# A two-layer hybrid decoder trunk on one core: limits of queued jobs, an earlier release, fixed places for two additions

## The chip, the cores and the metric

The kernel runs on one core of one Trainium2 chip. The metric is the device time of one execution in microseconds (us). Names of engines: PE is TensorE (matmul), PEld its weight load, DVE is VectorE, ACT is ScalarE, POOL is GpSimd, SP issues the DMAs.

## The reference, cut to what matters

The sequence has 256 positions of width 2048, all in float32, and there are two layers.

```
for l in range(DEPTH):
    h = rms_norm(x, mix_norm[l])
    z = h @ w_in[l]                                  # 2048 x 7168
    a_out = chunked_spatial_gating(z[..., :c_a], ...)          # gelu, layer norm, 128x128 mixing
    b_out = dilated_attention(z[..., c_a:c_q], z[..., c_q:c_k], z[..., c_k:], ...)
    mixed = concat([rms_norm(a_out, ...), rms_norm(b_out, ...)])
    x = x + mixed @ w_out[l]                         # 2048 x 2048
    h = rms_norm(x, ffn_norm[l])
    x = x + (silu(h @ w_gate[l]) * (h @ w_up[l])) @ w_down[l]  # 2048 x 5632, 5632 x 2048
```

## The kernel before, in words

Every matrix product is made at float32 accuracy from three matmuls of a rounded type: each operand is split into a high part (a copy on ACT) and a low part (source minus high part, on DVE), and `mm3` (line 837) adds high x high, high x low and low x high into one PSUM bank. The weights come from HBM as `raw` tiles by DMA and are split on the chip as well (`split_w`, line 815): tiles `wh` and `wl`, or `w` where both fit one slot. A weight item of 128 x 2048 thus takes one ACT copy and one DVE subtraction.

**Plain blocks.** The products with `w_in` and `w_out` go by blocks of 512 output columns (`plain_block`, line 844): two PSUM banks `Z`, one for each 128 positions, collect all slices of the contraction. Each slice is six matmuls. `w_out` is cut into halves "b" and "a" of the contraction; the last two blocks are (3,b) and (3,a). After each a residual operation adds the block, scaled by row, to `xs` (line 686) and gives its two banks back. After an "a" block the same job goes on: squares, transposes, and the operand of the FFN for these columns. Blocks 0 and 1 become the "forms" fF, blocks 2 and 3 the split tiles `fT`.

**Units.** The FFN's products go by `unit` (line 875). A gate/up unit makes 512 columns of gate and of up; a down unit makes two blocks of 512 columns of the result. A part of the contraction goes through a Strassen-like scheme with seven products instead of eight: seven sums of weight quarters, seven sums of operand quarters (the forms 11, 22, S1, S3, S2, 12, S4) and four banks called 1, X, Y and Z. The order of the seven is p1, p5, p6, p2, p7, p3, p4; a product has twelve matmuls in most units and six in the last chunk's down units. The tiles `e` and `raw` hold sums of weights. Between the products ACT copies banks (X from 1, Y from X, and the tiles s5 and s3, which the trace shows as `s`, as it does the silu tiles), and DVE adds s3 to Z and s5 to Y. The rest of the contraction follows as plain items of 24 matmuls that collect in the same four banks: banks 1 and X first (n = 0), then Y and Z (n = 1).

**Chunks.** The 11 blocks of the FFN's width go in chunks of 4, 4 and 3. A chunk has one gate/up unit for each block and then two down units. After a block's gate and up, ACT makes silu of the gate banks into two `t2` tiles, DVE multiplies them by the up banks, PE transposes the result (tiles `hTp`), and the transposes become the down units' operand (`Chunk.put_h`, line 705). Blocks 0 and 1 of a chunk go to a tile `xg`, and after block 1 its job makes the chunk's forms hF (and one fF) out of it, step by step (`make_forms`, line 618); for the third chunk also a rest `hR`. Blocks 2 and 3 become split tiles `hT`.

**What sets the order.** All instructions are emitted by a program that runs on the host and keeps a model of the queues (`Queues`, line 55): the time of PE, and that of ACT and DVE. Each engine then executes its own instructions in the emitted order, and only semaphores tie them together. The main loop goes through the items; before each it emits the weight preparation of later ones, as far as the ring allows (6 slots; an item takes two, or one in the last chunk's products), and then the item's matmuls. Everything else is a job, a generator that emits one step at a time. After each slice `run_jobs` looks at the jobs in the order of their limits, the highest first. A step is emitted when three things hold: the job's own model time plus 800 ns is past, its condition is met, and the backlog of ACT and DVE in the model is at most the job's limit:

```
def run_jobs(extra=0):
    for job in list(jobs):
        if job.t + MARGIN_NS <= q.pe and (job.when is None or job.when()):
            if q.backlog() <= job.limit + extra:
                job.step()
```

The limit is 4000 ns where none is given (`BACKLOG_NS`) and 30000 ns for the jobs of the FFN (`FFN_LIMIT`). Where the program needs something that a job has still to make, `drain` (line 233) moves the model's PE time on by 100 ns at a time and runs jobs until it is there. A `Lease` keeps the model's count of buffers: `mm_lease` of the four banks, `t2_lease` of the two silu tiles, `sd_lease` of the two banks for transposes.

Of the kernel before, what the change touches and what calls it, by code (L numbers as in the profile page):

```python
# [12 lines left out]
ALU = mybir.AluOpType  # L13
# [30 lines left out]
FFN_LIMIT = 30000  # L44
H_NS = 4000
MARGIN_NS = 800
BACKLOG_NS = 4000
# [95 lines left out]
def trunk_kernel(ctx: ExitStack, tc: tile.TileContext, aps: dict):  # L143
# [4 lines left out]
    dve = Engine(q, nc.vector, "dve", dve_cost)  # L148
# [52 lines left out]
    def pause(ns):  # L201
        q.chain = max(q.chain, q.pe) + ns
        yield
# [19 lines left out]
    def add(steps, limit=BACKLOG_NS):  # L223
        jobs.append(Job(steps, limit))
        jobs.sort(key=lambda job: -job.limit)
# [30 lines left out]
                    identity=ident)  # L256
        return tp

    def quad_T(src_of, put, g_of, name):

        yield from sd_lease.take(2)
        both = slot([P, 2, 4, SEQ], F32R, name)
        hi, lo = both[:, 0], both[:, 1]
        tps = [transpose_pair(src_of, 2 * pr, name + "p") for pr in range(2)]
        yield
        for pr in range(2):
            tp = tps[pr]
            if g_of is None:
                sl = slice(2 * pr, 2 * pr + 2)
                act.activation(out=hi[:, sl, :], in_=tp, func=ACTF.Copy)  # L270
                dve.tensor_tensor(
                    out=lo[:, sl, :], in0=tp, in1=hi[:, sl, :].bitcast(F32), op=ALU.subtract)
            else:
                for i in range(2):
                    k = 2 * pr + i
                    split_scaled(hi[:, k, :], lo[:, k, :], tp[:, i, :], g_of(k))
            sd_lease.give()
            if pr == 0:
                yield
        put(hi, lo)  # L280
# [318 lines left out]
        tiles = [slot([P, 2, 2, 4, P], F32R, name) for _ in range(n // 2)]  # L599
        return [t[:, h] for t in tiles for h in range(2)]  # L600

    def raw_T(src_of, dst, g_of, name):

        yield from sd_lease.take(2)
        tps = [transpose_pair(src_of, 2 * pr, name) for pr in range(2)]
        yield
        for pr in range(2):
            if g_of is None:
                act.activation(out=dst[:, 2 * pr:2 * pr + 2, :], in_=tps[pr], func=ACTF.Copy)
            else:  # L610
                for i in range(2):
                    k = 2 * pr + i
                    act.activation(
                        out=dst[:, k, :], in_=tps[pr][:, i, :], func=ACTF.Copy, scale=g_of(k))
            sd_lease.give()
            yield
# [81 lines left out]
    class Chunk:  # L698
# [3 lines left out]
            self.L, self.j0, self.n, self.s = L, j0, n, s  # L702
            self.table, self.F, self.xg = {}, None, None

        def put_h(self, j, src_of):
            i = j - self.j0
            if i >= 2:
                yield from quad_T(
                    src_of, lambda hi, lo: self.table.__setitem__(i, (hi, lo)), None, "hT")
                return  # L710
            if i == 0:
                self.xg = slot([P, 2, 4, SEQ], F32, "xg")
            yield from raw_T(src_of, self.xg[:, i], None, "hTp")
            if i == 1:
                s = self.s
                if s < 4:
                    both = slot([P, 2, 2, 4 - s, SEQ], F32R, "hR")
                    rest = self.xg[:, :, s:, :]
                    for h in range(2):
                        act.activation(out=both[:, 0, h], in_=rest[:, h], func=ACTF.Copy)  # L720
                        dve.tensor_tensor(
                            out=both[:, 1, h], in0=rest[:, h], in1=both[:, 0, h].bitcast(F32),
                            op=ALU.subtract)
                    yield
                    flat = both.rearrange("p a h k t -> p a (h k) t")
                    self.table["r"] = (flat[:, 0], flat[:, 1])
                F = Forms(form_halves(6, "hF") + [self.L.f_halves[7]], s)
                self.F = F
                yield from make_forms(F, self.xg)
# [12 lines left out]
    def gu_bank(L, j, chunk):  # L742

        s = {}

        def done(n, t, bank):
            if n == 0:
                yield lambda: hasattr(L, "r2")
                yield from t2_lease.take(1)
                s[t] = t2("s")  # L750
                act.activation(out=s[t], in_=bank, func=ACTF.Silu, scale=L.r2[:, t:t + 1])
                mm_lease.give()
                return
            yield lambda: t in s
            dve.scalar_tensor_tensor(
                out=s[t], in0=bank, scalar=L.r2[:, t:t + 1], in1=s[t], op0=ALU.mult, op1=ALU.mult)
            mm_lease.give()
            s["n"] = s.get("n", 0) + 1
            if s["n"] < NT:
                return  # L760
            yield from pause(H_NS)
            yield from chunk.put_h(j, lambda t: s[t])
            t2_lease.give(2)
        return done

    def down_bank(L, pair, chunk, last):
# [74 lines left out]
                out=out, lhsT=a, rhs=b, start=start and n == 0, stop=stop and n == 2,  # L841
                skip_group_check=True)

    def plain_block(src, kts, operand_of, done, first=None):

        st = {}
        for i in range(0, len(kts), KC):
            r = Raw([src[kts[i] // KC]], PLAIN_RAW)
            raws.append(r)
            for h in range(0, KC, HK):  # L850
                def prep(it, parts=1, r=r, h=h):
                    it.w = split_w(need(r)[:, h:h + HK, :], parts)
                    if h + HK == KC:
                        live[0] -= 1

                def run(it, i=i, h=h):
                    if i + h == 0:
                        if first is not None:
                            add(layer_consts(first), 20000)
                        drain(lambda: len(mm_lease.free) >= 2)  # L860
                        del mm_lease.free[:2]
                        st["Z"] = [mm_p.tile([P, W], F32, tag="mm", name=f"Z{t}") for t in range(NT)]
                    wh, wl = it.w
                    for k in range(HK):
                        n = i + h + k
                        for t in range(NT):
                            mm3(st["Z"][t], operand_of(kts[n], t), wh[:, k, :], wl[:, k, :],
                                n == 0, n == len(kts) - 1)
                        q.pe += 3 * NT * MM_NS
                        run_jobs()  # L870
                    if i + h + HK == len(kts):
                        add(done(st["Z"]))
                items.append(Item(1, PLAIN_RING, prep, run))

    def unit(s, quarter, plains, form, done):
# [6 lines left out]
        U = {}  # L882
# [74 lines left out]
        def r7(it):  # L957
            product(it, "S3", "X", False)
            copy(U["s3"], bank["X"])

            def sums():
                dve.tensor_tensor(out=bank["Z"], in0=bank["Z"], in1=U["s3"], op=ALU.add)
                yield lambda: "p3" in U
                yield from pause(0)
                dve.tensor_tensor(out=bank["Y"], in0=bank["Y"], in1=U["s5"], op=ALU.add)
                U["summed"] = True
            add(sums(), FFN_LIMIT)

        def r3(it):
            product(it, "S4", "Y", False)  # L970
            U["p3"] = True

        def r4(it):
            product(it, "22", "X", False)

        for p, r in ((p1, r1), (p5, r5), (p6, r6), (p2, r2), (p7, r7), (p3, r3), (p4, r4)):
            items.append(Item(1 if s <= 2 else 2, UNIT_RING, p, r))
# [3 lines left out]
        for i, (n, srcs, ops) in enumerate(plains):  # L981
            r = Raw(srcs, UNIT_RAW)
            raws.append(r)

            def prep(it, parts=1, r=r):
                it.w = split_w(need(r))
                live[0] -= 1

            def run(it, i=i, n=n, ops=ops):
                wh, wl = it.w  # L990
                for t in range(NT):
                    if n == 1:
                        drain(lambda: "summed" in U)
                    for k, op in enumerate(ops):
                        mm3(bank[names[n, t]], op(t), wh[:, k, :], wl[:, k, :], False, k == len(ops) - 1)
                        q.pe += 3 * MM_NS
                        run_jobs()
                    if i >= len(plains) - 2:
                        add(done(n, t, bank[names[n, t]]), FFN_LIMIT)
            items.append(Item(2, UNIT_RING, prep, run))  # L1000

    for l, L in enumerate(layers):
# [15 lines left out]
        for j, part in ((0, "b"), (1, "b"), (0, "a"), (1, "a"), (2, "b"), (2, "a"), (3, "b"), (3, "a")):  # L1018
            kts = list(range(8)) if part == "a" else list(range(8, 16))
            tab = operand(L.aT if part == "a" else L.bT)  # L1020
            plain_block(
                aps["w_out"][l, j], kts, (lambda kt, t, tab=tab: tab(kt % 8, t)), wout_done(L, j, part))
        j0 = 0
        for ci, (n, s) in enumerate(CHUNKS):
            chunk = Chunk(L, j0, n, s)
# [212 lines left out]
```

## Time and profile before

| | us |
|---|---|
| median of 3 runs | 2385.9 (2385.2 to 2387.07) |
| the profiled execution | 2385.62 |
| its span, first to last instruction | 2383.6 |
| PE busy | 2289.1 (96%) |
| weight load busy | 1878.5 (79%) |
| DVE busy | 1830.2 (77%) |
| ACT busy | 1325.7 (56%) |

The profile shows one execution. A busy PE includes matmuls at a lower granted clock, and the table of stretches has that clock in its own column. Line numbers of DVE and ACT instructions are those of the helper at line 90, which emits them all; the names of the tiles tell them apart (out, an arrow, in). Layer 0 runs from 0 to about 1200 us, layer 1 from there to the end; the FFN's first unit starts at 453.1 us in layer 0 and at 1644.8 us in layer 1.

### The profile page before, as it was taken

How to read it: one execution, taken by the hardware profiler on the slowest of the kernel's cores; microseconds unless marked ns; L12 is line 12 of the kernel's file. 1: busy time of each engine (PE TensorE's matmuls, PEld its weight loads, DVE VectorE, ACT ScalarE, POOL GpSimd, SP SyncE). 2: the span in 40 equal slices, each digit the busy share in tenths (PEclk: the TensorE clock that was granted, in tenths of full speed). 3: DMA queues.
4: the chain of work that ended last, by engine and by line, in shares of the span. 5: the costliest groups of instructions: out<-in, count | busy, mean ns of one | idle time of the engine just before them, and what ended most of it. 6: DMA issues, size and time to landing. Idle time of an engine off the chain costs nothing. (4 is left out here: it accounts for less than half of the span.)

```text
span 2383.6 us, 25937 instructions
## 1 busy us (share of the span) xinstructions
PE 2289.1 (96%) x10249; PEld 1878.5 (79%) x10249; DVE 1830.2 (77%) x1721; ACT 1325.7 (56%) x1590; POOL 52.5 (2%) x36
## 2 busy tenths in 40 slices
PE   9999999889999989999799999998899999899998
PEld 7888888677778878787688888886777788787876
DVE  6666766778798888988565666767787988889885
ACT  6556565455555655656355555654556556556462
POOL 0000000000000000000000000000000000000000
PEclk9999999999999999999999999999999999999999
DMA  8554455444465644645455444554445556346453
GB/s 350 185 177 159 161 201 204 155 145 159 179 227 189 228 148 160 263 159 194 163 182 196 152 162 170 195 212 158 142 159 180 226 191 228 146 161 262 159 194 106
DMA packets 66937, 440.33 MB, mean 185 GB/s; under 512 B 8064, under 2 KB 8576, under 8 KB 16768
## 3 DMA queue, kind: packets, MB, share of 16 engines
q1 hardware_dynamic: 66816, 438.69, 51.4%
q8 instruction: 80, 1.31, 0.2%
q14 instruction: 41, 0.34, 0.0%
HBM read 436.56 MB, written 2.10 MB: 184 GB/s over the span
## 5 line engine op out<-in xcount | busy, mean ns | idle before, releaser
L90 DVE TENSOR_TENSOR wl<-raw,wh 128x2048 fp32r<-128x2048 f32 x316 | 718.1, 2285 | 191.6 <-ACT wh L90 189.3
L90 ACT ACTIVATE wh<-raw 128x2048 fp32r<-128x2048 f32 x316 | 597.6, 1912 | 208.3 <-PE CX L840 76.5
L840 PE MATMUL Z<-w,xT 128*128 128x512 f32 x2688 | 640.6, 395 | 2.8 <-ACT w L90 1.5
L840 PEld LDWEIGHTS Z<-w,xT 128*128 128x128 f32 x2688 | 498.8, 188 | 106.9 <-ACT w L90 2.4
L90 DVE TENSOR_TENSOR w<-raw,w 128x1024 fp32r<-128x1024 f32 (+1 forms) x313 | 377.2, 1216 | 219.9 <-ACT w L90 215.0
L90 ACT ACTIVATE w<-raw 128x1024 fp32r<-128x1024 f32 (+1 forms) x313 | 316.2, 1049 | 47.8 <-DVE raw L90 29.5
L840 PE MATMUL CX<-wh,fF 128*128 128x512 f32 x528 | 174.8, 391 | 0.0
L840 PE MATMUL C<-wh,fF 128*128 128x512 f32 x352 | 130.0, 427 | 40.2 <-ACT s L90 23.0
L90 DVE TENSOR_TENSOR raw<-raw 128x2048 f32<-128x2048 f32 (+1 forms) x68 | 147.1, 2163 | 1.2
L840 PE MATMUL C<-wh,fT 128*128 128x512 f32 x352 | 117.3, 394 | 12.2 <-DVE fT L90 12.2
L840 PE MATMUL CY<-wh,fT 128*128 128x512 f32 x352 | 116.2, 391 | 2.7 <-DVE CY L90 2.7
L840 PEld LDWEIGHTS C<-wh,fF 128*128 128x128 f32 x352 | 72.7, 207 | 58.1 <-ACT s L90 24.7
L840 PE MATMUL CX<-wh,fT 128*128 128x512 f32 x352 | 117.6, 394 | 0.0
L840 PE MATMUL CZ<-wh,fT 128*128 128x512 f32 x352 | 115.5, 389 | 0.0
L840 PEld LDWEIGHTS CX<-wh,fF 128*128 128x128 f32 x528 | 99.2, 188 | 20.2
L840 PE MATMUL CX<-wl,fF 128*128 128x512 f32 x264 | 105.1, 398 | 4.5 <-DVE wl L90 4.4
L90 ACT ACTIVATE CX<-C 128x512 f32<-128x512 f32 x34 | 19.8, 582 | 151.7 <-PE C L840 151.7
L840 PE MATMUL Z<-w,bT 128*128 128x512 f32 x384 | 90.4, 392 | 0.0
L840 PE MATMUL Z<-w,aT 128*128 128x512 f32 x384 | 88.6, 390 | 0.0
L840 PEld LDWEIGHTS C<-wh,fT 128*128 128x128 f32 x352 | 66.8, 190 | 27.1 <-DVE fT L90 13.0
L840 PEld LDWEIGHTS Z<-w,aT 128*128 128x128 f32 x384 | 71.9, 188 | 14.9
L840 PEld LDWEIGHTS Z<-w,bT 128*128 128x128 f32 x384 | 71.7, 188 | 14.6
(192 smaller groups left out, 3554.8 us busy)
## 6 DMA issues: line engine op xcount, KB each, us to landing
raw<-in_w_in SPq DMA_DIRECT2D x109, 1024.0 KB, 4.8
raw<-in_w_gate SPq DMA_DIRECT2D x88, 1024.0 KB, 4.8
raw<-in_w_up SPq DMA_DIRECT2D x88, 1024.0 KB, 4.9
raw<-in_w_down SPq DMA_DIRECT2D x72, 1024.0 KB, 4.9
raw<-in_w_out SPq DMA_DIRECT2D x32, 1024.0 KB, 4.8
raw<-in_w_down SPq DMA_DIRECT2D x32, 512.0 KB, 4.1
raw<-in_w_in SPq DMA_DIRECT2D x5, 512.0 KB, 7.8
xstage<-in_xT SPq DMA_DIRECT2D x8, 256.0 KB, 7.3
```

Of the source, the lines that this page charges most:

```text
L90: return f(**kw)
L840: nc.tensor.matmul(out=out, lhsT=a, rhs=b, start=start and n == 0, stop=stop and n == 2, skip_group_check=True)
```

## The change

Four edits. The residual job of `w_out`, with all that follows it in the same job, gets the limit 30000 in place of 4000. `quad_T` and `raw_T` take a function `free` that they call when their transposes are emitted; the FFN's blocks give back the two silu tiles there, and not at the end of `put_h`. The job `sums` is gone: its two additions are emitted in the main order, Z's at the end of the sixth product's matmuls and Y's at the end of the seventh's. The drain that waited for the job before the plain items with n = 1 is gone with it.

```diff
-    def quad_T(src_of, put, g_of, name):
+    def quad_T(src_of, put, g_of, name, free=lambda: None):
...
         tps = [transpose_pair(src_of, 2 * pr, name + "p") for pr in range(2)]
+        free()
         yield
...
-    def raw_T(src_of, dst, g_of, name):
+    def raw_T(src_of, dst, g_of, name, free=lambda: None):
...
         tps = [transpose_pair(src_of, 2 * pr, name) for pr in range(2)]
+        free()
         yield
...
-        def put_h(self, j, src_of):
+        def put_h(self, j, src_of, free):
...
-                    src_of, lambda hi, lo: self.table.__setitem__(i, (hi, lo)), None, "hT")
+                    src_of, lambda hi, lo: self.table.__setitem__(i, (hi, lo)), None, "hT", free)
...
-            yield from raw_T(src_of, self.xg[:, i], None, "hTp")
+            yield from raw_T(src_of, self.xg[:, i], None, "hTp", free)
...
-            yield from chunk.put_h(j, lambda t: s[t])
-            t2_lease.give(2)
+            yield from chunk.put_h(j, lambda t: s[t], lambda: t2_lease.give(2))
...
-    def plain_block(src, kts, operand_of, done, first=None):
+    def plain_block(src, kts, operand_of, done, first=None, limit=BACKLOG_NS):
...
-                        add(done(st["Z"]))
+                        add(done(st["Z"]), limit)
...
             product(it, "S3", "X", False)
             copy(U["s3"], bank["X"])
 
-            def sums():
-                dve.tensor_tensor(out=bank["Z"], in0=bank["Z"], in1=U["s3"], op=ALU.add)
-                yield lambda: "p3" in U
-                yield from pause(0)
-                dve.tensor_tensor(out=bank["Y"], in0=bank["Y"], in1=U["s5"], op=ALU.add)
-                U["summed"] = True
-            add(sums(), FFN_LIMIT)
-
         def r3(it):
             product(it, "S4", "Y", False)
-            U["p3"] = True
+            w_sum(bank["Z"], bank["Z"], U["s3"], ALU.add)
 
         def r4(it):
             product(it, "22", "X", False)
+            w_sum(bank["Y"], bank["Y"], U["s5"], ALU.add)
...
-                    if n == 1:
-                        drain(lambda: "summed" in U)
...
-                aps["w_out"][l, j], kts, (lambda kt, t, tab=tab: tab(kt % 8, t)), wout_done(L, j, part))
+                aps["w_out"][l, j], kts, (lambda kt, t, tab=tab: tab(kt % 8, t)), wout_done(L, j, part),
+                limit=FFN_LIMIT)
```

`w_sum` (line 832) emits one DVE operation and leaves the model's chain time as it was.

## Rows read from the trace of the kernel before

**Rows 1.** The page, part 1: busy us (share of the span) and instructions.

```profile
PE 2289.1 (96%) x10249; PEld 1878.5 (79%) x10249; DVE 1830.2 (77%) x1721; ACT 1325.7 (56%) x1590; POOL 52.5 (2%) x36
```

**Rows 2.** List of waits of PE: us in total, times, longest.

```profile
PE C L840 <- ACT s L90: 26.2, 6, 5.8
PE CY L840 <- DVE CY L90: 19.6, 14, 5.1
PE C L840 <- DVE xs L90: 17.2, 2, 8.6
PE C L840 <- DVE fT L90: 12.2, 2, 6.1
PE CX L840 <- DVE wl L90: 7.8, 10, 0.8
```

**Rows 3.** Table of stretches: length, busy time of each engine, clock, DMA share, GB/s.

```profile
453.12:458.57 5.45, 5.45 (x13) 4.29 (x14) 1.82 (x3) 0.00 (x0) 0.00 (x0) 0.50 0.00 0
495.77:501.77 6.00, 6.00 (x17) 4.71 (x18) 0.72 (x3) 4.21 (x4) 0.70 (x1) 0.63 0.00 0
597.45:602.82 5.37, 5.37 (x13) 4.27 (x14) 1.42 (x3) 0.53 (x1) 0.00 (x0) 0.52 0.01 3
602.82:605.59 2.77, 2.77 (x13) 2.25 (x13) 0.23 (x1) 2.40 (x2) 0.00 (x0) 1.00 0.72 231
1138.69:1143.17 4.48, 4.48 (x13) 3.58 (x14) 3.34 (x3) 2.40 (x3) 0.00 (x0) 0.65 0.06 10
1169.83:1171.32 1.49, 1.49 (x6) 1.24 (x7) 0.00 (x0) 1.49 (x1) 0.00 (x0) 1.00 1.01 429
```

**Rows 4.** The same table: a unit without waits, then the one with forms.

```profile
507.05:549.04 41.99, 41.99 (x190) 34.53 (x188) 36.14 (x20) 24.70 (x19) 0.00 (x0) 1.00 0.53 188
549.04:597.45 48.41, 42.43 (x189) 34.27 (x187) 42.37 (x30) 28.28 (x26) 0.00 (x0) 0.98 0.48 174
```

**Rows 5.** DVE in order of time, FFN's entry: start, us, operation, [idle before <-releaser].

```profile
443.16 2.29 DVE L90 TENSOR_TENSOR wl<-raw,wh 128x2048 fp32r<-128x2048 f32 x1
...
446.80 0.69 DVE L90 TENSOR_TENSOR fF<-xg,fF 128x512 fp32r<-128x512 f32 x1 [0.76 <-ACT fF L90]
448.60 2.29 DVE L90 TENSOR_TENSOR wl<-raw,wh 128x2048 fp32r<-128x2048 f32 x1 [1.11 <-ACT wh L90]
...
452.23 1.40 DVE L90 SCALAR_TENSOR_TENSOR xs<-Z,rb,xs 128x512 f32<-128x512 f32 x2
453.55 1.40 DVE L90 SCALAR_TENSOR_TENSOR xs<-Z,ra,xs 128x512 f32<-128x512 f32 x2
```

**Rows 6.** DVE in order of time, before the first unit's plain items of fT.

```profile
495.24 0.48 DVE L90 SCALAR_TENSOR_TENSOR fT<-fTp,ffng,fT 128x256 fp32r<-128x256 f32 x1
496.26 0.48 DVE L90 SCALAR_TENSOR_TENSOR fT<-fTp,ffng,fT 128x256 fp32r<-128x256 f32 x1 [0.54 <-ACT fT L90]
```

**Rows 7.** DVE in order of time, between the third and fourth gate/up unit.

```profile
596.86 0.69 DVE L90 TENSOR_TENSOR fF<-xg,fF 128x512 fp32r<-128x512 f32 x1 [0.70 <-ACT fF L90]
...
598.12 0.74 DVE L90 SCALAR_TENSOR_TENSOR s<-CZ,r,s 128x512 f32<-128x512 f32 x1
605.36 2.29 DVE L90 TENSOR_TENSOR wl<-raw,wh 128x2048 fp32r<-128x2048 f32 x1 [6.49 <-ACT wh L90]
...
609.77 2.28 DVE L90 TENSOR_TENSOR wl<-e,wh 128x2048 fp32r<-128x2048 f32 x1
```

**Rows 8.** List of waits of PE from 1110 to 1190 us.

```profile
PE CY L840 <- DVE CY L90: 9.7, 2, 5.1
```

**Rows 9.** DVE in order of time, first down unit of the last chunk.

```profile
1129.86 0.69 DVE L90 TENSOR_TENSOR CZ<-CZ,s 128x512 f32<-128x512 f32 x1
...
1137.85 0.69 DVE L90 TENSOR_TENSOR CY<-CY,s 128x512 f32<-128x512 f32 x1
...
1148.66 0.69 DVE L90 TENSOR_TENSOR xs<-C,xs 128x512 f32<-128x512 f32 x1 [6.59 <-PE C L840]
```

**Rows 10.** DVE in order of time, start of the unit of 507.05 us.

```profile
512.47 2.29 DVE L90 TENSOR_TENSOR wl<-raw,wh 128x2048 fp32r<-128x2048 f32 x1 [4.25 <-ACT wh L90]
```

## The prediction, made before the changed kernel ran

> **What bounds the kernel now.** I read the page first: TensorE is busy for 96% of the span [rows 1], so what it lacks is 94.5 us. Who it waited for is told by the list of waits [rows 2]: ACT's "s" 26.2 us in 6 waits, the addition into bank Y 19.6 us in 14, the residual "xs" 17.2 us in 2, fT 12.2 us in 2. These four are 75 of the 94.5 us, and the diff touches what makes each. The third view is the table of stretches right behind such waits [rows 3]. Twelve matmuls take 2.77 us at granted clock 1.00 (2.4 GHz). Behind the 8.6 us wait for xs they take 5.45 us at clock 0.50 (1.2 GHz), behind a wait for s 5.37 us, behind a wait for bank Y 4.48 us at 0.65; behind a wait of 2.5 us six of them ran at 1.00. So each wait of some 5 us or more costs 1.7 to 2.7 us on top.
>
> The Trainium skill (Perfetto Trace Analysis, Identifying the Most-Contended Engine) says that matmul busy time is a poor measure of what TensorE could still give and that the busy share of weight loading is better. The page of the profile has 78.8% for that (1878.5 of 2383.6), a unit without waits 82.2% [rows 1, 4]. By the first measure 94.5 us are to be had; by the second 2383.6 - 1878.5 / 0.822 = 99 us. The trace has the difference in the half-clock stretches. Both stand above what I forecast.
>
> Behind TensorE stands DVE. A gate/up unit without waits takes 41.99 us with DVE busy for 36.1 of them; the unit in which a chunk's forms are made, with the wait behind it, takes 48.4, and DVE is busy for 42.4 [rows 4]. So near these waits DVE works almost without a break, and moving an operation ahead makes others late. That decides each size below.
>
> **The change, part by part.** Starts are us from the span's start, in layer 0; layer 1 has the same waits within 0.1 us unless told.
>
> *Residual at any backlog (17.2 us of wait).* At 444.5 (453.12 less 8.6) TensorE has ended w_out, and all four banks hold its last two blocks, (3,b) and (3,a). The next unit's first bank is that of (3,b), which its residual frees. This job is added when TensorE passes from (3,b) to (3,a), eight slices of six matmuls or 11 us earlier. By then DVE has been handed e, raw, wl and raw for the unit, up to the wl at 443.16 [rows 5], so the model's backlog is over 4000 ns, and the residual runs only at 452.23. With 30000 it goes in at the first step of (3,a), ahead of that wl; the last form step and half of fT's block 2, held back likewise, come along. What is late next: the second product needs the first bank of (3,a), and that residual is issued behind the wl of the third product. In DVE time from 443.2: form step 0.7 + 0.76 (wait for ACT) + 0.69, half of fT 2 x 0.48, residual (3,b) 1.40, two wl 4.58, half of residual (3,a) 0.70 = 9.8, so 453.0. Today the second product starts at 458.4 (453.12 + 5.45, less the overlap of two matmuls). I gain 5.4 and take off 0.7 for half clock: the wait left is about 5 us, which costs 1.7 as behind 1133.6, and today's half clock reaches some 1 us into that product. 4.7 per layer. Ends: 1 if the waits only change place and the clock drops twice, 11.5 if banks are never late (8.6 + 2.7 + 0.2). Two layers: **9.4**.
>
> *fT at any backlog (12.2 us).* fT's last block is finished at 496.74, its last two DVE operations (0.48 each) behind the unit's e, raw, wl, raw [rows 6]. With 30000 they are issued as soon as their transposes are made, before that group; the plain items that need them begin nine items, some 30 us of matmuls, after the start of the unit. So the 6.1 us goes, and the half clock behind it (16 matmuls in 6.00 us against 3.7: 2.3), 8.4 in all. Its four DVE operations then stand among the wl of the products, two with an ACT wait of 0.54 [rows 6]; I take off 1.1. 7.3 per layer; ends 4 (all four operations and one wl, 2.3, on the path) and 8.4. Two layers: **14.6**.
>
> *Silu tiles freed at the transposes.* Today the second block of a chunk keeps the two silu tiles until its forms are all made: TensorE ends the third unit at 591.7 (597.45 less 5.7), the forms end at 597.55 [rows 7], and only then ACT frees a bank. There are four such places, and two of 1.6 us where the next unit is a down unit (together the 26.2). After the change s is made right behind the gate's last matmul and TensorE goes straight on. The forms are still to be made, and DVE has no break until 598.86. What is late next is DVE's chain for the fourth and fifth products: wl at 605.36, which today waited 6.49 us because TensorE started late, raw, wl at 609.77 [rows 7]. From 598.86 on it can run 6.49 earlier, so the fifth product starts 6.5 earlier, not the 5.7 + 2.6 = 8.3 that go at the front; I take 6.1, since some form steps will fall behind that wl and meet ACT. About 2.2 us of wait are thus left at each place, short enough to keep the clock. Ends per place: 2.6 (6.3 less a wl, 2.3, and two steps of ACT and DVE, 2 x 0.7) and 8.3. Four places: **24.4**. At the two down places 1.6 is to be had and I take 1.0: **2.0** (ends 0 and 3.2).
>
> *Bank additions at a fixed place.* Z's addition stays where it is in DVE's order, as it was already issued during the sixth product. Y's moves. Today two more steps of its job have to come due, and in the last chunk two wl, half an hT, e and raw get in between: 1129.86 to 1137.85 [rows 9]. After the change it stands directly behind Z's in these short units (the ring of six admits no weight between) and is done at 1131.2, before TensorE wants it at 1133.6. What it pushes back by 0.69 is a wl needed some 8 us later, and DVE idles 6.59 us before xs at 1148.66 [rows 9]. So the two waits of 9.7 us go [rows 8] and in layer 1 one of 5 us (its second is 0.2), with 1.7 of half clock each; in the long units one wl is left in between, and the other 4.9 us of the 19.6 go in small pieces. 19.6 + 5.1 = 24.7; I take **23.5**, ends 18 and 24.7. The removed drain costs nothing on the chip: it emits no instruction.
>
> Sum: 9.4 + 14.6 + 24.4 + 2.0 + 23.5 = 73.9. The profiled execution took 2385.62 with a span of 2383.6; 2383.6 - 73.9 + 2.0 = 2311.7, so 2312. The median of the runs is 0.3 above that execution, which I neglect. All ends together: 38 (2347) and 101 (2285).
>
> **Rivals.** (1) *DVE is the bound.* All terms come out at their low ends: 2347. For it: DVE without a break at every place. Against: it idles 4 to 6.6 us in the next unit [rows 7, 9, 10]. (2) *The limit was not what held the jobs.* A step also wants its own model time to be 800 ns past and its condition met (line 229); if these held them, the first two terms fall away: 2385.6 - 49.9 = 2336. For it: Y's addition was held so, at a limit of 30000. Against: the residual's condition was met long before, and it ran where the model's backlog had sunk. (3) *Full cover.* DVE's idle time takes up what is moved: 2285 to 2293. Against it the sums at 453.0 and 605.4. (4) *Slower: the engine's head is blocked.* Behind the drain form steps ran close together; now their halves stand among wl and wh of the next unit, and each DVE half can wait for an ACT half that is queued behind a copy that waits for TensorE. A wl waits up to 4.25 us that way in a unit without TensorE waits [rows 10]. Four steps at six places at that price are 102 us, against the 36.6 that the six places lose today and the 47.5 of the other terms: 18 slower, 2404. It decides from 84 / 24 = 3.5 us per step; the two such waits in the rows are 0.76 and 0.70 [rows 5, 7].
>
> The Trainium skill (TensorE: Matmul & The Clock Gate, Architectural detail) says that ScalarE's and VectorE's queues are strictly first in, first out, which speaks against issuing at any backlog. The trace agrees: DVE stood 6.59 us before the xs at 1148.66, which waited for TensorE [rows 9]. By that rule alone rival 4 is what comes; by the rows above a step's wait is a fifth of the price it needs.
>
> **How the numbers follow.** Forecast (2297 to 2328): 62%. Rival 2: 12%, rival 1: 10%, rival 3: 8%, rival 4: 4%; 4% for a mixture that ends at no change. The range 2290 to 2348 holds the forecast, rivals 1 and 2, and a part of rival 3. About 0.2% (4.8 us) is what a measurement of this kernel can tell from no change: faster 0.92, same 0.04, slower 0.04.
>
> **What would show it.** In the waits: the 8.6 us wait for xs replaced by one of some 5 us or two of 2 to 3 us at the first products; fT gone; no wait over 3 us for s; CY under 2 us in all; waits for wl grown from 7.8 us [rows 2] to some 20. On DVE the residual at about 443 to 447 and Y's addition directly behind Z's in the last chunk. In the slices, clock under 0.95 at no more than the two w_out ends. I am wrong if DVE shows long waits for ACT's form halves, if wl waits pass 50 us, or if fT's last half still stands behind e and raw.

## The result

| | before, us | changed, us | ratio, 95% interval |
|---|---|---|---|
| first timing | 2385.6 (2384.7 to 2387.1) | 2309.0 (2307.8 to 2312.4) | 0.968 (0.966 to 0.970) |
| again, with the last experiments | 2387.4 (2383.4 to 2389.7) | 2310.1 (2309.7 to 2310.5) | 0.968 (0.967 to 0.969) |

The forecast was 2312. The time is right; two of the terms that make it up are not, in opposite directions, so that the nearness of the sum is in part luck. The experiments show that the three edits (the removed drain belongs to the additions) are not independent at all.

Part 1 of the page of the changed kernel, against [rows 1]:

```profile
PE 2267.2 (98%) x10249; PEld 1866.1 (81%) x10249; DVE 1829.9 (79%) x1721; ACT 1323.3 (57%) x1590; POOL 52.6 (2%) x36
```

The number of instructions on each engine is unchanged, and DVE works 1830 us as before. PE's busy time fell by 22 us with the same matmuls, since fewer of them ran at half clock; its idle time fell from 94.5 to 38.8 us. The busy time of weight load fell too, by 12 us, so the 99 us that the prediction worked out from it were no bound. The list of waits of PE of the changed kernel (us in total, times, longest), against [rows 2]:

```profile
PE CX L841 <- DVE wl L90: 12.1, 14, 0.9
PE C L841 <- DVE xs L90: 5.9, 2, 3.0
PE CY L841 <- ACT fF L90: 2.9, 2, 2.0
PE CX L841 <- ACT hF L90: 2.9, 2, 1.4
PE CX L841 <- ACT s L90: 2.5, 1, 2.5
PE CZ L841 <- DVE xs L90: 1.6, 2, 1.2
PE CX L841 <- DVE hF L90: 1.5, 2, 0.8
```

The waits for fT and for bank Y are gone, that for s is gone but for one place in layer 0's last chunk that was there before, that for xs fell from 17.2 to 7.5 us (two rows). New are 7.3 us for fF and hF, the forms; those for wl grew from 7.8 to 12.1, where I had expected some 20: the 2.2 us at each of the four places did not come. To see what each place gave, I read in both timelines when each unit's first matmul starts, and took the difference of how long a stretch lasts:

| stretch | layer 0, us shorter | layer 1, us shorter | my terms |
|---|---|---|---|
| end of w_out to the first unit's first matmul | 5.7 | 5.7 | |
| first unit | 8.5 | 8.8 | |
| second unit | -0.9 | -0.9 | entry: 12.0 per layer; measured 13.2 and 13.6 |
| chunk 1: third unit, fourth unit | 6.4, 2.5 | 6.4, 2.4 | 6.1 and a little for CY; measured 8.9, 8.8 |
| chunk 2: third unit, fourth unit | 6.4, 2.7 | 6.4, 2.6 | the same; measured 9.1, 9.0 |
| chunk 3: last gate/up unit | 2.9 | 2.9 | 1.0 and 0.85 for CY |
| chunk 3: first down unit | 1.9 | 1.3 | 6.8 |
| chunk 3: second down unit | 6.5 | 0.5 | 6.3 in layer 0, 0.2 in layer 1 |

Down units before the last chunk and the other gate/up units changed by less than 0.2 us. These are single executions: in a second one of the changed kernel, the first unit and the first down unit of the last chunk in layer 0 came out 0.5 us shorter and 0.9 longer, and the other rows the same within 0.1.

### The profile page after: what moved, and what is told of

The parts are those of the page before. It is cut to its first block, busy times and chain, and to the rows that moved or that the text cites. A ratio compares the mean times of both kernels' runs of the same rounds, so it can differ in the third digit from the quotient of the medians.

```text
span 2306.0 us, 25955 instructions
## 1 busy us (share of the span) xinstructions
PE 2267.2 (98%) x10249; PEld 1866.1 (81%) x10249; DVE 1829.9 (79%) x1721; ACT 1323.3 (57%) x1590; POOL 52.6 (2%) x36
## 4 chain that ended last, share of the span: by engine, by line
PE 89%; DVE 5%; ACT 2%; issue 2%; DMA 2%; SPq 0%; ACTq 0%; DVEq 0%
PE Z L841 32%; PE CX L841 18%; PE C L841 14%; PE CY L841 12%; PE CZ L841 10%; DVE wl L90 3%; ACT wh L90 1%; PE sc L463 1%; DVE raw L90 1%; PE hTp L254 1%; DMA gn<-in_k_norm 1%; PE qkp L254 1%; PE o L495 0%; ACT CX L90 0%; DMA raw<-in_w_in 0%
## 5 line engine op out<-in xcount | busy, mean ns | idle before, releaser
L90 ACT ACTIVATE w<-raw 128x1024 fp32r<-128x1024 f32 (+1 forms) x313 | 316.1, 1049 | 35.6 <-DVE raw L90 26.2
L841 PE MATMUL C<-wh,fF 128*128 128x512 f32 x352 | 122.3, 402 | 5.9 <-DVE xs L90 5.9
L841 PEld LDWEIGHTS C<-wh,fF 128*128 128x128 f32 x352 | 67.9, 193 | 20.6 <-issue 6.7
L841 PE MATMUL CY<-wh,fF 128*128 128x512 f32 x240 | 80.0, 392 | 0.0
```

The source lines that it names most:

```text
L90: return f(**kw)
L841: nc.tensor.matmul(out=out, lhsT=a, rhs=b, start=start and n == 0, stop=stop and n == 2, skip_group_check=True)
```

## The experiments

Each edit was run alone, in pairs, and then by parts. The two kernels of reference ran beside them.

**The limit alone.**

```diff
-                        add(done(st["Z"]))
+                        add(done(st["Z"]), limit)      # FFN_LIMIT for w_out, on the kernel before
```

> The kernel before with the residual jobs' limit of 30000 alone. Theory A (each edit takes away its own waits): the FFN's entry gains what the changed kernel gained there between the start of the first unit and the second, 13.2 us in layer 0 and 13.6 in layer 1, so 26.8 us: 2358.7 us; one wait for xs of 3 us and a second of 0.3 to 1.2 at the second product in each layer, fT gone, the waits for s and CY as before. Rival B (DVE is the bound and the edits need one another): the waits only move within the first unit, under 15 us gained, over 2370.

Measured: 2371.3 us against 2386.5, ratio 0.993 (0.992 to 0.995): 15 us, between the theories, nearer to B in time. PE's waits from 440 to 510 us, where the kernel before has 8.6 for xs and 6.1 for fT:

```profile
PE C L840 <- DVE xs L90: 3.0, 1, 3.0
PE CY L840 <- DVE CY L90: 2.6, 1, 2.6
PE CZ L840 <- DVE xs L90: 1.2, 1, 1.2
```

The waits of the entry went as the prediction has it. What is new is 2.6 us for Y's addition, which had not been waited for in this unit: on DVE six operations stand between Z's and Y's addition here, two in the kernel before. From w_out's end to the third unit the two layers gain 18 us in place of 26.8, and three down units of the last chunk are 1.2 to 1.5 us longer. So the waits of the residual and fT went, and Y's addition took part of the gain; what the last chunk lost, this run does not explain.

**The earlier release alone.**

```diff
-            yield from chunk.put_h(j, lambda t: s[t])
-            t2_lease.give(2)
+            yield from chunk.put_h(j, lambda t: s[t], lambda: t2_lease.give(2))
```

> The kernel before with the silu tiles' earlier release alone. Theory A: the four places in the gate/up units give 5.75 of wait and 2.5 to 2.9 of half clock each, 33.8 us, the two places before down units 1.6 each; in the last chunk's first down unit the forms now come late (1.4 + 0.8 + 2.0 us of waits for hF and fF), but PE then meets Y's addition that much later, so that the CY wait of 5 us shrinks instead: 37 us gained, 2348. Rival B (DVE takes most of it back, as my prediction's 24.4 + 2.0 had it): 26 us, 2359, with 2 us of new wl waits at each of the four places.

Measured: 2425.0 us against 2386.5, ratio 1.016 (1.014 to 1.017). Both theories missed: this edit by itself makes the kernel 39 us slower. Its waits of PE:

```profile
PE CY L841 <- DVE CY L90: 64.6, 18, 11.4
...
PE CX L841 <- ACT hF L90: 4.8, 2, 2.4
```

The waits for s at the four places are gone, but 64.6 us for bank Y have come in place of 19.6. DVE in order of time in the fourth unit (start, us, operation, idle before):

```profile
615.78 0.69 DVE L90 TENSOR_TENSOR CZ<-CZ,s 128x512 f32<-128x512 f32 x1
616.38 0.68 DVE L90 TENSOR_TENSOR hF<-xg,hF 128x512 fp32r<-128x512 f32 x1
616.98 4.67 DVE L90 TENSOR_TENSOR wl<-raw,wh 128x2048 fp32r<-128x2048 f32 x2
621.57 0.68 DVE L90 TENSOR_TENSOR hT<-hTp,hT 128x512 fp32r<-128x512 f32 x1
622.17 0.68 DVE L90 TENSOR_TENSOR xg<-xg 128x512 f32<-128x512 f32 x1
623.54 0.69 DVE L90 TENSOR_TENSOR fF<-xg,fF 128x512 fp32r<-128x512 f32 x1 [0.69 <-ACT fF L90]
625.35 2.29 DVE L90 TENSOR_TENSOR wl<-raw,wh 128x2048 fp32r<-128x2048 f32 x1 [1.11 <-ACT wh L90]
627.55 2.28 DVE L90 TENSOR_TENSOR e<-raw 128x2048 f32<-128x2048 f32 x1
629.87 2.29 DVE L90 TENSOR_TENSOR raw<-raw 128x2048 f32<-128x2048 f32 x1
632.08 0.69 DVE L90 TENSOR_TENSOR CY<-CY,s 128x512 f32<-128x512 f32 x1
```

Between Z's and Y's addition stand nine operations, and PE waits 11.4 us for the last line at four places. In these rows DVE itself waits 1.1 us at most; the order is simply wrong for PE. The third units of the first two chunks, where the wait for s was, gain 23.6 us together, and the fourth units lose 45.6. The first down unit of the last chunk is some 8 us longer in each layer, with waits for hF and fF ahead of the one for Y.

**The fixed additions alone.**

```diff
-            add(sums(), FFN_LIMIT)
...
+            w_sum(bank["Z"], bank["Z"], U["s3"], ALU.add)     # end of r3
...
+            w_sum(bank["Y"], bank["Y"], U["s5"], ALU.add)     # end of r4
```

> The kernel before with the bank additions at their fixed places alone. Theory A (the last chunk's gain of the additions is there, but in the changed kernel the late forms ate it): all CY waits go, 19.6 us, with three half-clock stretches of 1.7, less 0.7: 24 us gained, 2361.5, CY under 1 us in the list of waits. Rival C (the additions are not worth more than the changed kernel shows in its last chunks, 1.9 + 6.5 + 1.3 + 0.5, and 4.5 of small pieces): 15 us, 2371.

Measured: 2365.8 us, ratio 0.991 (0.990 to 0.992): 20.7 us, nearer to A. No wait for CY is left, and the first down unit of the last chunk is 6.8 us shorter in layer 0 and 3.9 in layer 1, where the changed kernel gained 1.9 and 1.3. What A overlooked is in the list of waits:

```profile
PE C L840 <- ACT s L90: 31.4, 6, 6.5
```

The wait for s was 26.2: it grew by 5.2, some 0.7 at each of the four gate/up places and 1.1 at the two down places. My reading is that PE comes that much earlier to a bank that is still held until the forms are made.

**Pairs.** The kernels of the next three are the changed one without its limit, the changed one without the earlier release, and the kernel before with limit and release.

```diff
# the changed kernel without the limit
-                aps["w_out"][l, j], ..., wout_done(L, j, part),
-                limit=FFN_LIMIT)
+                aps["w_out"][l, j], ..., wout_done(L, j, part))
# the changed kernel without the release
-            yield from chunk.put_h(j, lambda t: s[t], lambda: t2_lease.give(2))
+            yield from chunk.put_h(j, lambda t: s[t], lambda: None)
+            t2_lease.give(2)
```

> The changed kernel without the limit: release of the silu tiles and fixed additions together. After the release alone ran 39 us slower, theory D: it was slow only because Y's addition, a job then, fell some seven operations further back on DVE (64.6 us of CY waits, up to 11.4 each); with the fixed places the release gives its gain in full. The changed kernel less the 26.8 us that its entry gained: 2336. Rival E: the release costs of itself, by form steps among the weights of the next unit, and it was the earlier entry that gave DVE room: near or above the additions alone, 2366 or more.

> The changed kernel with the silu tiles held until the forms are made, as before. Theory D: the limit alone gave 15 us instead of 26.8 because Y's addition was late in the first unit as well (CY waits up from 19.6 to 24.9); with fixed additions its 26.8 come in full on top of the additions' 20.7: 2339. Rival E (the parts simply add): 15.2 + 20.7 = 36 us below before, 2350.

> The changed kernel without the fixed additions: limit and release on the kernel before. Theory D: still slower than before, as the release alone, with the 11 us waits for CY in the fourth unit of the first two chunks: 2425 less the limit's 15, 2410. Rival E (the earlier entry gives DVE the room): faster than before, 2360 or less.

Measured: 2335.7 us, ratio 0.978 (0.977 to 0.980); 2339.1 us, 0.980 (0.978 to 0.981); 2404.8 us, 1.007 (1.006 to 1.009). Theory D holds for all three, within 0.5 us for the first two and 5 for the third. In the third, PE still waits for Y's addition: 68.3 us in 20 waits, up to 11.4.

| | limit and release as before | limit | release | both |
|---|---|---|---|---|
| additions as a job | 2387 | 2371 | 2425 | 2405 |
| additions at fixed places | 2366 | 2339 | 2336 | 2309 |

With the additions as a job the limit is worth 15 and the release costs 39; with them at fixed places they are worth 27 and 30.

**What held Y's addition back.** The kernel with the release alone, and one line in its job:

```diff
                 dve.tensor_tensor(out=bank["Z"], in0=bank["Z"], in1=U["s3"], op=ALU.add)
+                q.chain = q.pe
                 yield lambda: "p3" in U
```

> The kernel with the release alone, but behind Z's addition the job that holds the two additions sets its own model time to that of PE, so that Y's step no longer waits until the model has DVE through with what is queued; it is a job still, and nothing else is changed. Theory D, sharpened: the job's own time is what held Y's addition back; on DVE it then comes two places behind Z's in the long units, and the time falls from 2425 to that of release and fixed additions within 6 us, about 2340. Rival F (being a job, behind the forms and hT jobs in the list, is what counts): it stays over 2400.

Measured: 2337.9 us, ratio 0.979 (0.978 to 0.981), against 2425.0 without the line and 2335.7 with the fixed places. Theory D holds. The same stretch of DVE in this kernel:

```profile
611.84 0.69 DVE L90 TENSOR_TENSOR CZ<-CZ,s 128x512 f32<-128x512 f32 x1
612.44 0.68 DVE L90 TENSOR_TENSOR hF<-xg,hF 128x512 fp32r<-128x512 f32 x1
613.04 2.29 DVE L90 TENSOR_TENSOR wl<-raw,wh 128x2048 fp32r<-128x2048 f32 x1
615.25 0.69 DVE L90 TENSOR_TENSOR CY<-CY,s 128x512 f32<-128x512 f32 x1
```

So it was neither the limit (it was 30000 all along) nor the place among the jobs. A job's next step is emitted only when the model has DVE through with its last one; the longer DVE's queue in the model, the later the step, and by then more weights have been queued ahead. That the wait for the silu tiles had hidden this in the kernel before is read from the program and not shown by a run: the drain there moves the model's PE time on until the tiles are free in the model, and by then DVE's queue in the model is short.

**The forms of the last chunk.** The changed kernel, with the tiles of the third chunk's block 1 held as before.

```diff
+            late = chunk.n == 3 and j - chunk.j0 == 1
+            yield from chunk.put_h(
+                j, lambda t: s[t], (lambda: None) if late else (lambda: t2_lease.give(2)))
+            if late:
+                t2_lease.give(2)
```

> The changed kernel, but in the third chunk block 1 gives its silu tiles back only after its forms, as in the kernel before. Theory A: the form waits of the last chunk's first down unit go (4.2 us in layer 0, 3.1 and 1.5 of half clock in layer 1), the 1.6 us wait for s before it comes back in each layer: 5.6 us faster than the changed kernel, 2303.4. Rival B (DVE is the bound there): the same time as the changed kernel within 1.5 us, the waits at other tiles.

Measured: 2308.9 us, ratio 0.967 (0.966 to 0.969), not to be told from the changed kernel; rival B has the time right. From 1080 to 1125 us PE's only wait is one of 2.7 us for s, where the changed kernel has 4.2 us for hF and fF. The form waits went, as theory A says, and the first down unit is 4.9 us shorter in layer 0 and 3.9 in layer 1, but the kernel does not keep it: the wait that comes back is 2.7 and not 1.6, and makes the unit ahead 2.9 us longer in each layer, and in layer 0 the second down unit gave 1.6 back.

**Two steps further.** Beside a repeated run of the changed kernel: the fourth product's weight sum behind the fifth product's split, and the last residual emitted at the end of its block.

```diff
# the weight sum, from p2 to p7
             it.w = split_w(need(b21))
-            w_sum(b11.tile, b21.tile, b11.tile, ALU.subtract)
-            live[0] -= 1
...
             it.w = split_w(U["e"])
-            live[0] -= 1
+            w_sum(b11.tile, b21.tile, b11.tile, ALU.subtract)
+            live[0] -= 2
# the residual of (3,a)
                         add(done(st["Z"]), limit)
+                        if at_once:        # (j, part) == (3, "a"): its two steps now
+                            job.step(); job.step()
```

> The changed kernel again, beside the three that follow: 2309 us, within 2.

> The changed kernel, with the fourth product's weight sum behind the fifth product's weight split on DVE. Theory G: the 14 waits of 0.8 to 0.9 us for wl at the fifth product (12.1 us in all) come from the chain wl, raw, wl of 2.3 each on DVE, and the sum in its middle is not needed before the seventh product: the waits go, some 0.3 of each comes back at the sixth product, 6 to 8 us faster, 2302. Rival B (DVE is the bound there): the wait moves to the sixth product in full, 2309.

> The changed kernel, with the residual of the last block (3,a) emitted at the block's end, ahead of the third product's weight split. Theory G: the second product waits for the bank of (3,a), whose residual stands behind a wl of 2.3 on DVE; it starts 2.2 us earlier in each layer, the third product's weights come 1.4 later and are still in time: 4 us faster, 2305. Rival B: the wait moves from the second to the third product, 2309.

Measured: 2307.3 us (ratio 0.967, 0.965 to 0.968) and 2308.8 us (0.967, 0.966 to 0.968), against 2310.1 (0.968, 0.967 to 0.969) for the changed kernel beside them. Neither can be told from it; rival B has the time right in both. With the sum moved, the wait went whole from the fifth product to the sixth, 0.84 us each in most units as before: the list of waits has 12.2 us in 16 waits of CY for wl where the changed kernel has 12.1 us in 14 of CX. The equal time hides two larger changes, though. The wait for xs at the second product grew to 2.8 us, and the FFN's first unit is 2.5 and 3.6 us longer in the two layers; the second down unit of the last chunk in layer 0 is 5.1 us shorter.

With the residual moved, PE's waits from 440 to 500 us are these; the changed kernel beside it has 3.0 and then 1.3 for xs at the second product:

```profile
PE C L841 <- DVE xs L90: 3.0, 1, 3.0
PE CX L841 <- DVE wl L90: 0.8, 1, 0.8
PE C L841 <- DVE wl L90: 0.6, 1, 0.6
```

**All of it.** The changed kernel with these two edits and the tiles of the third chunk held.

> The changed kernel with the last two edits and with the third chunk's silu tiles held until its forms are made. Theory G: the gains add, 1.9 + 7 + 4: 2296. Rival B: 2307, as the held tiles alone.

Measured: 2301.0 us (2299.2 to 2303.8), ratio 0.964 (0.963 to 0.965), the fastest kernel here; its interval lies just below that of the changed kernel beside it. Between the theories: 9 us below the changed kernel, where G said 13. The profiled executions lie 6 us apart. Unit by unit, the two down units of the last chunk in layer 0 are 8.5 us shorter together and the first one in layer 1 is 2.6; the gate/up unit ahead of them is 2.8 longer in each layer, and the FFN's first unit some 1 us. In the down units of layer 0 the changed kernel waits for s, CY, hF and fF, 7.2 us together; here only 2.8 for s is left of the waits from 1085 to 1160 us. The single edits tell which did that. With the sum moved alone, the second down unit takes 32.5 us as here, against 37.6 in the changed kernel, without a wait for s or CY; how the moved sum does that stays open. With the tiles held alone, the first one takes 32.3, here 34.7, against 38.1.

## Why the prediction was right, and where its steps were not

**The residual and fT.** Right. The second product was forecast to start at 453.0, 8.5 us after w_out's end, when the bank of (3,a) comes free. It starts 8.8 after. DVE of the changed kernel in the same stretch as [rows 5]:

```profile
443.66 0.69 DVE L90 TENSOR_TENSOR xg<-xg 128x512 f32<-128x512 f32 x1
445.04 0.69 DVE L90 TENSOR_TENSOR fF<-xg,fF 128x512 fp32r<-128x512 f32 x1 [0.70 <-ACT fF L90]
445.65 0.48 DVE L90 SCALAR_TENSOR_TENSOR fT<-fTp,ffng,fT 128x256 fp32r<-128x256 f32 x1
446.67 0.48 DVE L90 SCALAR_TENSOR_TENSOR fT<-fTp,ffng,fT 128x256 fp32r<-128x256 f32 x1 [0.54 <-ACT fT L90]
447.07 1.40 DVE L90 SCALAR_TENSOR_TENSOR xs<-Z,rb,xs 128x512 f32<-128x512 f32 x2
448.47 4.49 DVE L90 TENSOR_TENSOR wl<-raw,wh 128x2048 fp32r<-128x2048 f32 x2
452.88 1.40 DVE L90 SCALAR_TENSOR_TENSOR xs<-Z,ra,xs 128x512 f32<-128x512 f32 x2
```

This is the list that the prediction added up, in order, and DVE has hardly a break in it. The wait is split in two, 3.0 before the first product and, before the second, 0.4 in layer 0 and 1.2 in layer 1. fT's last half is done at 479.5 and no one waits for it; that DVE is the bound at this place is what the kernel with the residual at once showed.

**The silu tiles.** The mechanism right, the size wrong: 24.4 forecast for four places, some 35 measured (35.9 by the table, less about a quarter of a microsecond of CY at each). The step that failed is "about 2.2 us of wait are thus left at each place". I let all form steps pass DVE before the weights of the fourth product. DVE of the changed kernel, to be held against [rows 7]:

```profile
581.70 0.68 DVE L90 TENSOR_TENSOR xg<-xg 128x512 f32<-128x512 f32 x1
582.30 0.68 DVE L90 TENSOR_TENSOR hF<-xg,hF 128x512 fp32r<-128x512 f32 x1
583.76 2.29 DVE L90 TENSOR_TENSOR wl<-raw,wh 128x2048 fp32r<-128x2048 f32 x1 [0.78 <-ACT wh L90]
...
588.17 2.29 DVE L90 TENSOR_TENSOR wl<-e,wh 128x2048 fp32r<-128x2048 f32 x1
590.37 0.68 DVE L90 TENSOR_TENSOR hF<-xg,hF 128x512 fp32r<-128x512 f32 x1
...
598.45 0.68 DVE L90 TENSOR_TENSOR hF<-xg,hF 128x512 fp32r<-128x512 f32 x1
```

The steps come one at a time, some 8 us apart, and find room: one (xg and hF) before the fourth product's wl, which waits 0.78 us for ACT, one behind the fifth product's, one before Z's addition. No unit of chunks 1 and 2 shows a wait for forms, and the table of stretches of the changed kernel has the unit with forms and the one behind it, against [rows 4], at full clock and full speed:

```profile
536.30:578.34 42.04, 42.04 (x190) 34.53 (x188) 36.66 (x24) 26.89 (x23) 0.00 (x0) 1.00 0.54 200
578.34:620.42 42.08, 42.08 (x190) 34.46 (x188) 39.24 (x27) 24.87 (x22) 0.00 (x0) 1.00 0.56 200
```

**The bank additions.** Y's addition moved as forecast, right behind Z's in the last chunk's down units and with one to three operations between in the others, and no wait for CY is left. Alone this gave 20.7, not 23.5, as the wait for s took some back. In the changed kernel the down units of the last chunk gained 10.2 us by the table, where my terms for them add up to 20.1. DVE and PE's waits there, against [rows 9] and [rows 8] (first the operations, then the waits from 1075 to 1140 us):

```profile
1089.20 0.75 DVE L90 TENSOR_TENSOR hF<-xg,hF 128x256 fp32r<-128x256 f32 x2
...
1096.78 0.43 DVE L90 TENSOR_TENSOR fF<-xg,fF 128x256 fp32r<-128x256 f32 x1 [0.48 <-ACT fF L90]
...
1101.88 0.69 DVE L90 TENSOR_TENSOR CZ<-CZ,s 128x512 f32<-128x512 f32 x1
1102.48 0.69 DVE L90 TENSOR_TENSOR CY<-CY,s 128x512 f32<-128x512 f32 x1
```

```profile
PE CY L841 <- ACT fF L90: 2.0, 1, 2.0
PE CX L841 <- ACT hF L90: 1.4, 1, 1.4
...
PE CX L841 <- DVE hF L90: 0.8, 1, 0.8
```

This unit needs the forms at once, and the drain that had made them all in time is gone with the wait for the tiles: 4.2 us of waits for hF and fF. I had given this place a gain of 1.0 and no loss. So what these terms overlooked is what would be late next here: the forms. By the table the last chunk gave 16.0 us in place of some 24, the four places 35.9 in place of 24.4 and about 1 for CY, the entry 26.8 in place of 24.0. The first two errors nearly cancel, which is luck, and so 2312 came out at 2309.

**The rivals.** Rival 4 (slower) missed its mechanism and not its danger. Halves of form steps wait 0.5 to 0.7 us for ACT on DVE, as [rows 5, 7] had it. But the release alone is 39 us slower, by the order in which jobs are emitted. Rival 2 had the right rule, a step's own model time, at the wrong job: it did not hold the residual, it held Y's addition, which the prediction had noted without asking what the release would do to it. My sum treated the terms as independent, and they were so only because the fixed additions were part of the change.

**The clock.** I took some 2.2 us of wait to be "short enough to keep the clock", from a wait of 2.5 us behind which it stayed at 1.00. Stretches of the changed kernel behind a wait of 2.97 us, one of 2.54 us, and two of 1.4 and 0.8 us in a row:

```profile
447.96:453.42 5.46, 5.46 (x12) 3.78 (x12) 5.46 (x4) 2.27 (x2) 0.00 (x0) 0.50 0.21 90
1134.63:1136.12 1.49, 1.49 (x7) 1.23 (x7) 0.00 (x0) 1.49 (x1) 0.00 (x0) 1.00 0.95 401
2238.81:2243.50 4.69, 4.69 (x14) 3.69 (x14) 0.46 (x1) 2.40 (x2) 0.00 (x0) 0.64 0.35 109
```

The first fell to half (1.2 GHz), the second did not, the third partly did. Behind the same two waits of 1.4 and 0.8 us in layer 0 the clock stayed at 1.00 (1090.01 to 1094.80 us), and in the second execution of the changed kernel it fell to 0.60 there. At the first product the half clock cost PE 2.7 us (5.46 against 2.77) and the kernel nothing: the second product waits for DVE and starts 8.8 us after w_out's end in layer 0 and in layer 1, where the first product ran at 0.63 in 4.59 us and the wait behind it was longer. The 0.7 us that I took off for half clock at the second product were hardly lost either: the stretch from w_out's end to its start is 5.3 us shorter, against the 5.4 of the prediction.

## What to carry to other kernels

Where a host program emits the order, a wait can be load-bearing: the wait for the silu tiles cost some 35 us at four places, and yet the kernel became 39 us slower when it alone was taken away, because Y's addition was then emitted later. So look, for each wait that goes, at what is emitted while the program waits, and give an operation that PE needs next a fixed place in the order rather than a place in a queue. Where one engine has hardly a break, as DVE at the FFN's entry, add up its operations in their order up to the one that PE waits for: that sum was right to 0.3 us, whereas guesses at what "falls behind" were not.

## What the runs showed of the hardware that was not expected

A wait of 2.97 us on TensorE was followed by 5.46 us at half clock, one of 2.54 us by none, and two of 1.4 and 0.8 us in a row by a stretch at 0.64. The same two waits in the other layer of the same execution left it at 1.00. So the length of a wait does not tell alone whether the clock falls. And half clock need not cost time: at the FFN's first product, 5.46 us at 0.50 and 4.59 us at 0.63 led to the same start of the second product, 8.8 us after w_out's end, since that one waits for DVE.
